# Queries of mixer B's second pair projected beside the last block's norm, high parts first in the feed-forward parts, and queries of mixer B split on POOL

## The chip, the core and the metric

The kernel runs on one core of a Trainium2 chip. The core has a matrix engine (TensorE, PE in the profile), three engines for elementwise work (VectorE or DVE, ScalarE or ACT, GpSimd or POOL), a queue engine that starts transfers (SyncE or SP), and 16 DMA engines. PE has a matmul row (PE) and a weight-load row (PEld). Each engine works through its own list of instructions in a fixed order; semaphores tie the lists together. The metric is device microseconds (us) of one execution, and lower is better. Medians of several runs are compared.

## What is computed

One layer of a streaming encoder for 1024 prompt frames and 32 sample frames, width 1024, in float32:

```python
h = adaln_in(x, gains[0], sh1, sc1)
x = x + FFN_RES * g1[:, None] * rmsnorm(swiglu(h, w1_gate, w1_up, w1_down), gains[1])
h = adaln_in(x, gains[2], sh2, sc2)
qa, ka, va, qb, kb, vb = jnp.split(h @ w_in, SPLITS, axis=-1)
oa, ob, rows = mixers(qa, ka, va, qb, kb, vb)
o = jnp.concatenate([rmsnorm(oa, ...), rmsnorm(ob, ...)], axis=-1) @ w_out
x = x + g2[:, None] * rmsnorm(o, gains[3])
h = adaln_in(x, gains[4], sh3, sc3)
x = x + FFN_RES * g3[:, None] * rmsnorm(swiglu(h, w2_gate, w2_up, w2_down), gains[5])
```

`swiglu(h) = (silu(h @ w_gate) * (h @ w_up)) @ w_down` with 2816 inner columns. Mixer A has 8 heads of 64 over 576 keys, mixer B has 8 query heads on 2 key heads with a window of 128 and a learned sink per head.

## The kernel before

The 1056 frames are held transposed (features on partitions, frames along the columns) in three **blocks** `tb` of 384, 384 and 288 columns. A float32 product is made of three faster matmuls: each operand is a high part plus a low part, and `mm3` (L324) issues, for one slice `k` of 128 features, weight-high times frame-high (L325), weight-high times frame-low (L326) and weight-low times frame-high (L327). `split_w` (L299) loads 128 weight columns, ACT copies out the high part (L303), DVE subtracts for the low part (L304). `norm_h` (L409) makes the two frame parts: DVE multiplies by the row factors into `n` (L420), ACT adds the shift and rounds to `h_hi` (L444), and the low part `h_lo` is made on DVE (L446) or, for every fourth slice, on POOL (L449). Ahead of it `mean_rstd` (L396) sums squares: ACT squares, POOL and DVE fold (`sq`, L368, L370), PE adds over partitions (`pss`, L357), DVE takes the inverse root (`rv`, `ry`, L334 to L391) and PE spreads it (`pr`, L405).

The stages are: first feed-forward part (`ffn`, key "h1"; in it `up(ff, tb)` makes the `gate` and `up` products of 128 inner columns, 24 matmuls each, and `down` the `dn` products); the norm `h2` and mixer B's keys, values and first queries, block by block (loop at L1077); attention; the output projection `wo`; second feed-forward part (key "h3").

In the attention stage 36 pieces for mixer B (32 `TileB`, 4 `TileS`) and 36 for mixer A run one after another. A `TileB` is two heads by 128 frames: `pre` (L796) clears part of a buffer `qs` on POOL (L799) and calls `split_q` (L716), which writes two copies of the query's high part (L721 or L723) and its low part (L724) for each of the two heads; `qk` makes the scores `Sb` (L813, L814), `tr` the transposes `ppb`, `av` the product with the values `po`. `SPLIT = "vav"` names the engines of the three writes: DVE, ACT, DVE. `TileS` are the sample frames' pieces (scores `Ss`). The four query projections of mixer B are `qk_proj` pieces (`pq`), 24 matmuls for each block: pair 0 is made in the loop at L1077, pairs 1 to 3 are the first units of `flows[0]`, whose work is spread as filler between the attention pieces 0 to 34, at a rate that is the units' summed cost over the pieces.

The order on each engine is fixed before the run by a scheduler: it gives earlier program steps priority and puts a later step ahead where it expects the earlier one to wait. Buffers come from pools by tag: `u` (6 buffers of block size, `u_tile`), `w` (8, weights), `r` (3, raw loads), `h` (5, among them `n`, `qs` and the transposed probabilities). PSUM has three banks for `p1` (gate, up, pv, pq, wo), two pairs for `p2` (dn, S, Sb, Ss) and one bank for `pc` (pss, pr, pk, po).

```python
                    for k in range(KT):
                        mm3(ps[s][:, :w], wgu[ff][s], k, hi[:, k, :], lo[:, k, :], k == 0, k == KT - 1)
```

Of the kernel before, what the change touches and what calls it, by code (L numbers as in the profile page):

```python
# [8 lines left out]
F32R = mybir.dt.float32r  # L9
# [8 lines left out]
KT = D // 128  # L18
# [40 lines left out]
PFILL = 5  # L59
KEARLY = 1  # L60
KB = 0
SPLIT = "vav"
LEAD_B = 2
MANUAL = False
WAIT = 3
# [1 line left out]
STAGES = ((0, 34), (37, 54))  # L67
# [7 lines left out]
def encoder_step(ctx: ExitStack, tc, x_prompt, x_sample, cache_a_k, cache_a_v, cache_b_k, cache_b_v,  # L75
# [4 lines left out]
    te, ve, ae, ge, dma = nc.tensor, nc.vector, nc.scalar, nc.gpsimd, nc.sync  # L80
# [215 lines left out]
        return bs  # L296


    def split_w(src):  # L299
        r = rpool.tile([128, 8, 128], F32, name="raw", tag="r")  # L300
        dma.dma_start(r, src)
        w = wpool.tile([128, 2, 8, 128], F32R, name="w", tag="w")
        ae.activation(w[:, 0], r, AF.Copy)  # L303
        ve.tensor_sub(w[:, 1], r, w[:, 0])  # L304
        return w

    def split_cols(wm, c):
        return split_w(wm[0, :, 128 * c:128 * c + 128].rearrange("(k p) n -> p k n", p=128))

    def split_rows(wm, r):  # L310
        return split_w(wm[0, 128 * r:128 * r + 128, :].rearrange("p (k n) -> p k n", n=128))
# [12 lines left out]
    def mm3(ps, w, k, hi, lo, start, stop):  # L324
        te.matmul(ps, w[:, 0, k], hi, start=start, stop=False)  # L325
        te.matmul(ps, w[:, 0, k], lo, start=False, stop=False)  # L326
        te.matmul(ps, w[:, 1, k], hi, start=False, stop=stop)  # L327


    def rsqrt(v, n, m):  # L330
# [170 lines left out]
    def need(key):  # L501
        while key not in done:
            step(1)
# [21 lines left out]
    def ffn(key, H, F, wg, wu, wd, per_group, key_out, after, beside=lambda ff, tb: None):  # L525
        late, pre = [], {}
        plan = rounds(*ROUNDS[key])
        begun = set()
        final = {tb: max(i for i, (g, t) in enumerate(plan) if tb in t) for tb in range(3)}

        def load(r, ff):
            pre[r, ff] = (split_cols(wg, ff), split_cols(wu, ff))

        load(0, 0)
        yield
        for r, (gi, blocks) in enumerate(plan):
            grp = GROUPS[gi]
            wgu, wds, gs = {}, {}, {}

            def up(ff, tb):  # L540
                need((key, tb))
                w = TB[tb][1]
                hi, lo = H[tb]
                ps = [p1("gate"), p1("up")]
                for s in range(2):
                    for k in range(KT):
                        mm3(ps[s][:, :w], wgu[ff][s], k, hi[:, k, :], lo[:, k, :], k == 0, k == KT - 1)
                    step(FAST if gi == 0 else PACE)
                sl = s_tile([128, 384], "sl")
                ae.activation(sl[:, :w], ps[0][:, :w], AF.Silu)  # L550
                ve.tensor_tensor(sl[:, :w], sl[:, :w], ps[1][:, :w], op=OP.mult)  # L551
                g = g_tile([128, 2, 384], "gg", F32R)
                ae.activation(g[:, 0, :w], sl[:, :w], AF.Copy)
                ve.tensor_sub(g[:, 1, :w], sl[:, :w], g[:, 0, :w])  # L554
                gs[ff, tb] = g
                beside(ff, tb)
                if late:
                    late.pop()()

            def down(tb, r=r, grp=grp, wds=wds, gs=gs):  # L560
                w = TB[tb][1]
                new = tb not in begun
                begun.add(tb)
                if new:
                    F[tb] = u_tile(tb, "facc", F32)
                if r == final[tb]:
                    if key_out != "y" or tb == 0:
                        finish()
                    own = marked((key_out, tb), after(tb))
                for mp in range(KT // 2):  # L570
                    ps = p2("dn")
                    for s in range(2):
                        for i, ff in enumerate(grp):
                            g = gs[ff, tb]
                            mm3(ps[:, s, :w], wds[ff], 2 * mp + s, g[:, 0, :w], g[:, 1, :w],
                                i == 0, i == len(grp) - 1)
                    o = F[tb][:, 2 * mp:2 * mp + 2, :]
                    if new:
                        ve.tensor_copy(o, ps[:, :, :w])
                    else:  # L580
                        ve.tensor_tensor(o, ps[:, :, :w], o, op=OP.add)  # L581
                    if r == final[tb]:
                        next(own)
                    step(1)
                if r == final[tb]:
                    side.append(own)

            x, y = grp
            if r:
                load(r, x)  # L590
            load(r, y)
            if r == XAT and key == "h1":
                XIN[1] = load_x(1)
            wgu.update({x: pre[r, x], y: pre[r, y]})
            for ff in grp:
                wds[ff] = split_rows(wd, ff)
            for tb in blocks:
                up(x, tb)
                up(y, tb)
                if len(begun) < 2:  # L600
                    down(tb)
                else:
                    late.append(lambda down=down, tb=tb: down(tb))
            if (gi, 2) == (gi, blocks[-1]):
                per_group(gi)
        late.pop()()
# [87 lines left out]
    def run(gen):  # L694
        for _ in gen:
            pass
# [378 lines left out]
        dma.dma_start(nbv_s[0, 0].rearrange("t h d -> t (h d)"), kvbs[:, 128:256])  # L1075

    for tb in range(3):  # L1077
        need(("h2", tb))
        if tb == 0:
            keys_cached()  # L1080
        for x in token_tiles(tb):
            run(kv_piece(*x))
        if tb == 2:
            KSB = wpool.tile([128, 2, 1024], F32R, name="KSB", tag="w")
            if PRIME:
                primed.append(load_qb(1))
            keys = [lambda: keys_new(0, 4), lambda: keys_new(4, 4), keys_sample]
        if tb == 2 and KEARLY == 1:
            keys.pop(0)()
        run(q0_piece(tb))  # L1090
        for i, x in enumerate(token_tiles(tb)):
            run(v0_piece(*x))
            if tb == 2 and KEARLY:
                keys and keys.pop(0)()
# [27 lines left out]
    def unit_qb(p):  # L1122
        return [(("B", p), lambda: load_qb(p), lambda w: flow_qb(p, w))]

    def unit_va(g):
        return [(("V", g), lambda: load_va(g), lambda w: flow_va(g, w))]

    def unit_qka(p):
        return [(("K", p), lambda: load_ka(p), lambda w: flow_ka(p, w)),
                (("A", p), lambda: load_qa(p), lambda w: flow_qa(p, w))]  # L1130

    flows = [(*STAGES[0], unit_qb(1) + unit_qb(2) + unit_qb(3) + unit_va(1) + unit_qka(0)),
             (*STAGES[1], unit_qka(1) + unit_qka(2) + unit_qka(3))]
    COST = {"B": 10.6, "V": 23.4, "K": 10.6, "A": 10.6}

# [78 lines left out]

        return LEAD_B if t < 36 else 1

    ready.add(("B", 0))
    todo = []
    for t in range(N):
        at = max(-1, t - lead(t))  # L1220
# [12 lines left out]
    with tc.manual_schedule(engines={mybir.EngineType.PE}) if MANUAL else ExitStack():  # L1233
        waits[0] = WAIT
        preps += [prepare(*key) for key in opens[0]]
        scores(-1, 1)
        if PRIME == 2:
            now = flow(flows[0][2])
            fill(PFILL)
# [116 lines left out]
```

## Time and profile before

| | before |
|---|---|
| median of 3 runs | 2216.33 us (2215.64 to 2218.37) |
| the profiled execution | 2217.6 us, its span 2215.8 us |
| granted TensorE clock, mean | 0.984 of full speed |
| PE busy | 2161.6 us (98%) |
| DVE, ACT, POOL busy | 1239.1 us (56%), 697.8 us (31%), 179.2 us (8%) |

The span is what lies between the first and the last instruction; 1.8 us of the profiled execution lie around it. PE is busy nearly throughout, so a microsecond counts where PE waits, where it runs at the lower of its two clock levels, or where work on it is removed. A wait stands in square brackets in the timeline, with what ended it. "PEclk" is the granted clock of a stretch, 1.00 being full speed (2.4 GHz) and 0.50 the lower level (1.2 GHz); a value between them is a stretch that had both.

### The profile page before, as it was taken

The numbers are of one execution on the slowest core, as the hardware profiler recorded it, in microseconds if no ns is written. First come the engines' busy times: TensorE is split into PE (matmuls) and PEld (weight loads), VectorE is DVE, ScalarE is ACT, GpSimd is POOL, SyncE is SP. The second block draws the span as 40 slices with busy tenths as digits, with TensorE's granted clock in tenths as the row PEclk, the third lists the DMA queues.
The fourth block names the chain that finished last, engine by engine and source line by source line (L and its number), as shares of the span: only waits on it lengthen the run. The fifth ranks groups of instructions, "written<-read, shape, count | busy, mean of one in ns | idle before, by whom it ended". The sixth has DMA issues, their size and how long they took to land.

```text
span 2215.8 us, 33976 instructions
## 1 busy us (share of the span) xinstructions
PE 2161.6 (98%) x14012; PEld 2068.6 (93%) x14012; DVE 1239.1 (56%) x2425; ACT 697.8 (31%) x1450; POOL 179.2 (8%) x281
## 2 busy tenths in 40 slices
PE   6999999999999999899999899999999999999998
PEld 4999999999999999799787589999999999999998
DVE  5788667874333497677444865785333333333336
ACT  4411111111121253576444663542111111111133
POOL 1100000000000023001110313220000000000000
PEclk8999999999999999899999899999999999999999
DMA  9253334434122352111112121424211111111122
GB/s 323 93 153 118 111 96 124 143 101 129 39 66 69 101 184 93 38 39 30 50 30 62 46 77 67 134 86 120 66 58 39 57 39 39 58 38 58 39 69 79
DMA packets 200623, 186.03 MB, mean 84 GB/s; under 512 B 7597, under 2 KB 169813, under 8 KB 199317
## 3 DMA queue, kind: packets, MB, share of 16 engines
q1 hardware_dynamic: 200468, 183.87, 27.1%
q8 instruction: 110, 1.80, 0.3%
q14 instruction: 45, 0.36, 0.1%
HBM read 164.12 MB, written 22.86 MB: 84 GB/s over the span
## 4 chain that ended last, share of the span: by engine, by line
PE 90%; DVE 4%; DMA 3%; ACT 1%; issue 1%; POOL 0%; SPq 0%; ACTq 0%; DVEq 0%; POOLq 0%
PE dn L325 7%; PE dn L326 7%; PE dn L327 7%; PE gate L327 7%; PE gate L326 7%; PE up L327 7%; PE up L326 7%; PE gate L325 7%; PE up L325 7%; PE po L713 3%; PE S L752 2%; PE pq L325 2%; PE pq L327 2%; PE pq L326 2%; DMA raw<-in_w_gate_dram 1%; PE pp L776 1%
## 5 line engine op out<-in xcount | busy, mean ns | idle before, releaser
L326 PE MATMUL gate<-h_lo,w 128*128 128x384 f32 (+1 forms) x1056 | 340.2, 322 | 4.0 <-DVE h_lo L446 4.0
L325 PE MATMUL dn<-gg,w 128*128 128x384 f32 (+1 forms) x1056 | 341.4, 325 | 1.1 <-DVE facc L581 1.0
L581 DVE TENSOR_TENSOR facc<-dn,facc 128x768 f32<-128x768 f32 (+1 forms) x240 | 212.9, 889 | 230.2 <-PE dn L327 229.9
L326 PE MATMUL dn<-gg,w 128*128 128x384 f32 (+1 forms) x1056 | 340.6, 323 | 0.6 <-DVE gg L554 0.6
L325 PE MATMUL gate<-h_hi,w 128*128 128x384 f32 (+1 forms) x1056 | 341.0, 323 | 0.0
L327 PE MATMUL gate<-h_hi,w 128*128 128x384 f32 (+1 forms) x1056 | 340.4, 322 | 0.0
L325 PE MATMUL up<-h_hi,w 128*128 128x384 f32 (+1 forms) x1056 | 340.2, 322 | 0.0
L326 PE MATMUL up<-h_lo,w 128*128 128x384 f32 (+1 forms) x1056 | 340.0, 322 | 0.0
L327 PE MATMUL dn<-gg,w 128*128 128x384 f32 (+1 forms) x1056 | 340.0, 322 | 0.0
L327 PE MATMUL up<-h_hi,w 128*128 128x384 f32 (+1 forms) x1056 | 339.9, 322 | 0.0
L304 DVE TENSOR_TENSOR w<-raw,w 128x1024 fp32r<-128x1024 f32 x187 | 231.5, 1246 | 150.5 <-ACT w L303 150.3
L303 ACT ACTIVATE w<-raw 128x1024 fp32r<-128x1024 f32 x187 | 195.7, 1056 | 266.1 <-PE dn L327 103.5
L550 ACT ACTIVATE sl<-gate 128x384 f32<-128x384 f32 (+1 forms) x132 | 60.9, 462 | 563.9 <-PE gate L327 560.9
L551 DVE TENSOR_TENSOR sl<-sl,up 128x384 f32<-128x384 f32 (+1 forms) x132 | 68.5, 519 | 292.1 <-PE up L327 286.1
L326 PEld LDWEIGHTS gate<-h_lo,w 128*128 128x128 f32 x1056 | 198.6, 188 | 4.6 <-DVE h_lo L446 4.6
L325 PEld LDWEIGHTS dn<-gg,w 128*128 128x128 f32 x1056 | 199.2, 189 | 1.6 <-DVE facc L581 1.2
L326 PEld LDWEIGHTS dn<-gg,w 128*128 128x128 f32 x1056 | 199.2, 189 | 1.0 <-DVE gg L554 0.9
L327 PEld LDWEIGHTS dn<-gg,w 128*128 128x128 f32 x1056 | 199.1, 189 | 0.0
L325 PEld LDWEIGHTS gate<-h_hi,w 128*128 128x128 f32 x1056 | 198.7, 188 | 0.1
L327 PEld LDWEIGHTS gate<-h_hi,w 128*128 128x128 f32 x1056 | 198.7, 188 | 0.0
L327 PEld LDWEIGHTS up<-h_hi,w 128*128 128x128 f32 x1056 | 198.7, 188 | 0.0
L325 PEld LDWEIGHTS up<-h_hi,w 128*128 128x128 f32 x1056 | 198.5, 188 | 0.0
(224 smaller groups left out, 3367.4 us busy)
## 6 DMA issues: line engine op xcount, KB each, us to landing
raw<-in_w_mod_dram SPq DMA_DIRECT2D x56, 512.0 KB, 4.0
raw<-in_w_gate_dram SPq DMA_DIRECT2D x54, 512.0 KB, 4.0
raw<-in_w_up_dram SPq DMA_DIRECT2D x54, 512.0 KB, 4.7
raw<-in_w_down_dram SPq DMA_DIRECT2D x54, 512.0 KB, 4.5
raw<-in_w_in_dram SPq DMA_DIRECT2D x18, 512.0 KB, 4.3
wm<-in_w_mod_dram SPq DMA_DIRECT2D x8, 1024.0 KB, 7.4
raw<-in_w_out_dram SPq DMA_DIRECT2D x13, 512.0 KB, 4.5
xr<-xs SPq DMA_DIRECT2D x16, 384.0 KB, 3.5
```

The lines of the kernel that those rows point to most:

```text
L303: ae.activation(w[:, 0], r, AF.Copy)
L304: ve.tensor_sub(w[:, 1], r, w[:, 0])
L325: te.matmul(ps, w[:, 0, k], hi, start=start, stop=False)
L326: te.matmul(ps, w[:, 0, k], lo, start=False, stop=False)
L327: te.matmul(ps, w[:, 1, k], hi, start=False, stop=stop)
L550: ae.activation(sl[:, :w], ps[0][:, :w], AF.Silu)
L551: ve.tensor_tensor(sl[:, :w], sl[:, :w], ps[1][:, :w], op=OP.mult)
L581: ve.tensor_tensor(o, ps[:, :, :w], o, op=OP.add)
L713: te.matmul(po[64 * h:64 * h + 64, :n], vsl(j, h, kn), PT(h, j, kn), start=j == 0, stop=j == nt - 1)
L752: te.matmul(S[:, c:ce], self.T[:, h, :], KQ[:, 0, 128 * k0 + c:128 * k0 + ce], start=True, stop=True)
L776: te.transpose(pp[:, j - j0, :], P[:, 128 * j:128 * j + 128], ident)
```

## The change

Three edits. `up` no longer calls `mm3` per slice but `mm_all`: for all eight slices weight-high and weight-low times frame-high, and after them weight-high times frame-low; the 24 matmuls are the same. Pair 1 of mixer B's queries is taken out of `flows[0]`: its weights are loaded in the loop at L1077 ahead of the wait for the third block's norm, into a buffer of the pool `u` (named `wu`), blocks 0 and 1 are projected there, and block 2 after the first scores of the attention stage. `SPLIT = "ggg"` puts all three writes of `split_q` on POOL.

```diff
-SPLIT = "vav"
+SPLIT = "ggg"
...
-    def split_w(src):
+    def split_w(src, pool=None):
         r = rpool.tile([128, 8, 128], F32, name="raw", tag="r")
         dma.dma_start(r, src)
-        w = wpool.tile([128, 2, 8, 128], F32R, name="w", tag="w")
+        if pool is None:
+            w = wpool.tile([128, 2, 8, 128], F32R, name="w", tag="w")
+        else:
+            w = pool.tile([128, 2, 8, 128], F32R, name="wu", tag="u", bufs=6)
         ae.activation(w[:, 0], r, AF.Copy)
         ve.tensor_sub(w[:, 1], r, w[:, 0])
         return w
...
+    def mm_all(ps, w, hi, lo):
+
+        for k in range(KT):
+            te.matmul(ps, w[:, 0, k], hi[:, k, :], start=k == 0, stop=False)
+            te.matmul(ps, w[:, 1, k], hi[:, k, :], start=False, stop=False)
+        for k in range(KT):
+            te.matmul(ps, w[:, 0, k], lo[:, k, :], start=False, stop=k == KT - 1)
...
                 for s in range(2):
-                    for k in range(KT):
-                        mm3(ps[s][:, :w], wgu[ff][s], k, hi[:, k, :], lo[:, k, :], k == 0, k == KT - 1)
+                    mm_all(ps[s][:, :w], wgu[ff][s], hi, lo)
                     step(FAST if gi == 0 else PACE)
...
     for tb in range(3):
+        if tb == 2:
+            q1_piece = start_qb(1, split_cols(w_in, 13, upool))
+            for b in range(2):
+                for _ in q1_piece(b):
+                    step(2)
         need(("h2", tb))
...
-    flows = [(*STAGES[0], unit_qb(1) + unit_qb(2) + unit_qb(3) + unit_va(1) + unit_qka(0)),
+    flows = [(*STAGES[0], unit_qb(2) + unit_qb(3) + unit_va(1) + unit_qka(0)),
...
-    ready.add(("B", 0))
+    ready |= {("B", 0), ("B", 1)}
...
         scores(-1, 1)
+        run(q1_piece(2))
```

How the order moves, at three places. **First**, PE at the start of block 1 in the first feed-forward part, right behind the `dn` products of block 0 (`gate_771`, `up_772` and `gate_827` are three PSUM banks, `h_hi_456` and `h_lo_457` block 1's parts). Before:

```order
L325 MATMUL gate_771<-h_hi_456,w_258 128x384
L325 MATMUL up_772<-h_hi_456,w_263 128x384
L325 MATMUL gate_827<-h_hi_456,w_315 128x384
L326 MATMUL gate_771<-h_lo_457,w_258 128x384
L327 MATMUL gate_771<-h_hi_456,w_258 128x384
```

Now:

```order
L335 MATMUL gate_771<-h_hi_456,w_258 128x384
L336 MATMUL gate_771<-h_hi_456,w_258 128x384
L335 MATMUL up_772<-h_hi_456,w_263 128x384
L336 MATMUL up_772<-h_hi_456,w_263 128x384
L335 MATMUL gate_827<-h_hi_456,w_315 128x384
L336 MATMUL gate_827<-h_hi_456,w_315 128x384
```

Three matmuls stood ahead of the first low part; now 36 on high parts and 20 `dn` matmuls do. The second feed-forward part has the same two orders at its block 1, with other buffer numbers.

**Second**, PE at the end of the loop at L1077 (`pv_7977` is the last value product of block 1, `pss_7670`, `pr_7759` the sums and factors of block 2's norm, `h_hi_7789` its output). Before:

```order
L671 MATMUL pv_7977<-w_7467,h_lo_7136 128x256
L357 MATMUL pss_7670<-ones_98,sq_7700 128x1 x2
L357 MATMUL pss_7670<-ones_98,sq_7700 32x1
L357 MATMUL pss_7670<-ones_98,sq_7736 128x1 x2
L357 MATMUL pss_7670<-ones_98,sq_7736 32x1
L405 MATMUL pr_7759<-ident_96,ry_7747 128x128 x2
L405 MATMUL pr_7759<-ident_96,ry_7747 128x32
L669 MATMUL pv_8003<-w_7447,h_hi_7789 128x256
```

Now, around the sums:

```order
L330 MATMUL pq_8009<-h_hi_6700,wu_8005 128x384
L328 MATMUL pq_8035<-h_hi_7135,wu_8005 128x384
L368 MATMUL pss_7670<-ones_98,sq_7700 128x1 x2
L368 MATMUL pss_7670<-ones_98,sq_7700 32x1
L368 MATMUL pss_7670<-ones_98,sq_7736 128x1 x2
L368 MATMUL pss_7670<-ones_98,sq_7736 32x1
L329 MATMUL pq_8035<-h_lo_7136,wu_8005 128x384
L330 MATMUL pq_8035<-h_hi_7135,wu_8005 128x384
```

and around the factors:

```order
L329 MATMUL pq_8035<-h_lo_7136,wu_8005 128x384
L330 MATMUL pq_8035<-h_hi_7135,wu_8005 128x384
L416 MATMUL pr_7759<-ident_96,ry_7747 128x128 x2
L416 MATMUL pr_7759<-ident_96,ry_7747 128x32
L679 MATMUL pv_8061<-w_7447,h_hi_7789 128x256
```

25 of the 48 moved matmuls stand ahead of the sums, 23 between the sums and the factors. Behind the factors PE's order is as before: six `pv` on the first high parts, then `pk`.

**Third**, POOL around the same norm (`qs` are the split queries of the first attention pieces). Before:

```order
L799 MEMSET qs_8245 64x256
L449 TENSOR_TENSOR h_lo_7790<-n_7830,h_hi_7789 128x256
L449 TENSOR_TENSOR h_lo_7790<-n_7830,h_hi_7789 128x32
L799 MEMSET qs_8273 64x256
L799 MEMSET qs_8301 64x256
L449 TENSOR_TENSOR h_lo_7790<-n_7910,h_hi_7789 128x256
```

Now:

```order
L809 MEMSET qs_8303 64x256
L733 CAST qs_8303<-qbt_7472 64x128 x4
L734 TENSOR_TENSOR qs_8303<-qbt_7472,qs_8303 64x128 x2
L460 TENSOR_TENSOR h_lo_7790<-n_7830,h_hi_7789 128x256
L460 TENSOR_TENSOR h_lo_7790<-n_7830,h_hi_7789 128x32
L809 MEMSET qs_8331 64x256
L733 CAST qs_8331<-qbt_7472 64x128 x4
L809 MEMSET qs_8386 64x256
L733 CAST qs_8386<-qbt_7472 64x128 x4
L460 TENSOR_TENSOR h_lo_7790<-n_7910,h_hi_7789 128x256
```

Each piece now has seven POOL instructions where it had one, and two pieces' copies stand ahead of block 2's last low part.

## Rows read from the trace of the kernel before

**Rows 1.** Page, part 1: the matmul row and the weight loads, busy us and counts.

```profile
PE 2161.6 (98%) x14012; PEld 2068.6 (93%) x14012; DVE 1239.1 (56%) x2425; ACT 697.8 (31%) x1450; POOL 179.2 (8%) x281
```

**Rows 2.** Windows: stretch, length, busy PE, PEld, DVE, ACT, POOL, then PEclk, DMA, GB/s.

```profile
75.00:80.00 5.00, 5.00 (x22) 5.00 (x21) 5.00 (x7) 1.88 (x3) 2.58 (x3) 0.67 0.01 3
885.00:900.00 15.00, 9.53 (x55) 8.47 (x55) 11.75 (x45) 8.43 (x27) 3.33 (x7) 0.66 0.00 0
920.00:925.00 5.00, 4.47 (x18) 3.90 (x19) 4.34 (x15) 3.28 (x14) 0.31 (x1) 0.66 0.17 55
1440.00:1450.00 10.00, 7.87 (x37) 7.55 (x36) 10.00 (x14) 5.57 (x10) 3.80 (x4) 0.83 0.11 29
920.00:1063.00 143.00, 141.53 (x1109) 128.26 (x1109) 107.47 (x382) 99.03 (x348) 11.45 (x40) 0.99 0.10 29
```

**Rows 3.** PE timeline (start, us, instruction, wait) where block 1 starts, both feed-forward parts.

```profile
71.73 0.34 PE L325 MATMUL up<-h_hi,w 128*128 128x384 f32 x1
71.90 0.34 PE L325 MATMUL gate<-h_hi,w 128*128 128x384 f32 x1
74.07 0.45 PE L326 MATMUL gate<-h_lo,w 128*128 128x384 f32 x1 [1.83 <-DVE h_lo L446]
...
1440.46 0.34 PE L325 MATMUL gate<-h_hi,w 128*128 128x384 f32 x1
1442.92 0.45 PE L326 MATMUL gate<-h_lo,w 128*128 128x384 f32 x1 [2.13 <-DVE h_lo L446]
```

**Rows 4.** DVE timeline ahead of the first of these two waits.

```profile
68.66 4.29 DVE L420 SCALAR_TENSOR_TENSOR n<-xt,acoef,pr 128x384 f32<-128x384 f32 x8
72.86 1.16 DVE L446 SCALAR_TENSOR_TENSOR h_lo<-n,modT,h_hi 128x384 fp32r<-128x384 f32 x1
```

**Rows 5.** PE timeline at block 2's norm, then at the first attention scores.

```profile
884.45 1.34 PE L357 MATMUL pss<-ones,sq 128*128 128x1 f32 x12
888.24 1.75 PE L405 MATMUL pr<-ident,ry 128*128 128x128 f32 x6 [2.44 <-DVE ry L338]
891.11 0.58 PE L669 MATMUL pv<-w,h_hi 128*128 128x256 f32 x1 [1.11 <-ACT h_hi L444]
...
894.66 1.08 PE L1057 MATMUL pk<-ident,vt 128*128 128x128 f32 x4 [1.91 <-DVE n L420]
...
917.93 0.22 PE L877 MATMUL Ss<-KB2s,qbs 64*32 64x32 f32 x2
920.53 0.39 PE L813 MATMUL Sb<-KSB,qs 128*128 128x256 f32 x1 [2.38 <-ACT Ps L888]
```

**Rows 6.** DVE timeline at block 2's norm.

```profile
884.19 0.46 DVE L370 TENSOR_TENSOR sq<-sq 128x288 f32<-128x288 f32 x1
885.83 0.16 DVE L388 TENSOR_SCALAR rv<-pss 128x2 f32<-128x2 f32 x1 [1.19 <-PE pss L357]
...
890.03 4.49 DVE L420 SCALAR_TENSOR_TENSOR n<-facc,acoef,pr 128x256 f32<-128x256 f32 x16 [1.94 <-PE pr L405]
```

**Rows 7.** Page, part 5: the split of weights on DVE, busy us and mean ns.

```profile
L304 DVE TENSOR_TENSOR w<-raw,w 128x1024 fp32r<-128x1024 f32 x187 | 231.5, 1246 | 150.5 <-ACT w L303 150.3
```

**Rows 8.** Who writes `qs`: ns min/median/max, first and last start, forms.

```profile
L721 ACT ACTIVATE qs<-qbt x64: 307/309/312, 891.3 to 1053.6; 64x128 fp32r<-64x128 f32 x64
L723 DVE CAST qs<-qbt x64: 198/223/652, 895.0 to 1052.3; 64x128 fp32r<-64x128 f32 x64
L724 DVE TENSOR_TENSOR qs<-qbt,qs x64: 260/285/720, 898.2 to 1053.0; 64x128 fp32r<-64x128 f32 x64
```

**Rows 9.** POOL by line and shape: busy us, mean ns, idle before.

```profile
L742 POOL COPY qz<-KQ 64x128 f32<-64x128 f32 x64 | 22.9, 358 | 2.8
L799 POOL MEMSET qs<- 64x256 f32 x32 | 10.2, 318 | 141.9 <-PE po L713 68.8 <-PE Sb L814 44.6 <-ACT vt L673 4.2
L449 POOL TENSOR_TENSOR h_lo<-n,h_hi 128x256 fp32r<-128x256 f32 x6 | 5.4, 903 | 51.5 <-ACT n L448 51.5
L449 POOL TENSOR_TENSOR h_lo<-n,h_hi 128x32 fp32r<-128x32 f32 x6 | 2.3, 377 | 0.0
```

More of the change, by code (lines that the diff above doesn't have):

```diff
@@ L305, in split_w, with split_cols @@
         return w
-    def split_cols(wm, c):
-        return split_w(wm[0, :, 128 * c:128 * c + 128].rearrange("(k p) n -> p k n", p=128))
+    def split_cols(wm, c, pool=None):
+        return split_w(wm[0, :, 128 * c:128 * c + 128].rearrange("(k p) n -> p k n", p=128), pool)
     def split_rows(wm, r):
```

## The prediction

> **What bounds the kernel now.** I read the page's busy times first. PE is busy 2161.6 of 2215.8 us [rows 1], so a change pays only where PE waits, where it runs at the lower clock, or where work beside a wait is moved. Next, the windows show the stretches with a clock below 1.00 [rows 2], and in them the PE timeline shows which wait stands there. Three kinds of place bear on the change. Block 1 of both feed-forward parts waits 1.83 and 2.13 us for a low part [rows 3]. Block 2's norm before attention has waits of 2.44, 1.11 and 1.91 us in fifteen microseconds, and the start of attention one of 2.38 us [rows 5]. The rest of mixer B's stage has next to none: 141.53 of 143 us busy at 0.99 of full clock, with DVE at 107.47, ACT at 99.03 and POOL at 11.45 us [rows 2]. A lower clock costs twice: over 5 us busy at 0.67, 5.00 × 0.33 = 1.65 us of full-speed work is lost beside the wait itself.
>
> **High parts first.** At block 1 PE issues three matmuls on the high part and then needs the low part's first slice, which DVE makes only when its eight products `n` are through (4.29 us), 1.16 us a slice [rows 4]; so PE waits 1.83 us. Afterwards 36 matmuls on high parts and 20 `dn` stand ahead of it. Two matmuls of 384 columns start 71.90 − 71.73 = 0.17 us apart [rows 3], so the 36 alone last 36 × 0.172 = 6.2 us, three times the wait. DVE, which makes six of the eight low parts (POOL the two others) at 1.16 us each or less, began them at 72.86, so they are through by about 80; PE's 36 and the 20 `dn`, 9.6 us in all from 71.7 on, reach past that. What is late next: the last high parts, made by ACT slice after slice; the 20 `dn` lie among them. Gain: the wait and the lost clock, 1.83 + 1.65 = 3.5 us, and in the second part 2.13 + 7.87 × 0.17 = 1.3, 3.4 us. **Together −7.** The number of matmuls is the same. At the very first block, which has no `dn` work, 24 high matmuls stand ahead of the lows in place of few; a wait there could shrink or grow by about the size of those above; I take nothing and keep ±2 for the range.
>
> **The second pair's queries: out of the filler.** 48 matmuls of 384 columns and 24 of 288 leave the stage of mixer B: 48 × 0.172 = 8.3, 24 × 0.172 × 0.75 = 3.1 us, in sum **−11.4** if PE limits that stage, as 141.53 of 143 us says [rows 2]. The filler is thinner for it: the rate is the units' cost over the pieces. The stage would be some 131.5 us, in which DVE would be busy for 107 and ACT for 99 even if the split stayed on them. PE stays the bound. I put 1 us against it for waits that thinner filler lets through (between 0 and 6): **−10.4**.
>
> **Into the norm hole.** 25 of the 48 stand ahead of the sums `pss`, which start at 884.45, right behind DVE's last fold (884.19 + 0.46 = 884.65) [rows 5, 6]. They begin 25 × 0.172 = 4.3 us later. Then 23 × 0.172 = 4.0 us stand between `pss` and the factors `pr`, where PE waited 2.44: the chain from `pss` through `rv` and `ry` is covered. `pr` so starts at 884.45 + 4.3 + 1.3 + 4.0 ≈ 894, in place of 888.24. Behind `pr` nothing changed: DVE's `n` (4.49 us [rows 6]) follow `pr`, and PE waits 1.11 and 1.91 us as before. `pr` took 1.75 us for six, at the lower clock; having run without a stop ahead, it may now take half, −0.9. So `pk` starts at 894 + (894.66 − 888.24) − 0.9 ≈ 899.4 instead of 894.66: **+4.7** for 8.3 us of moved work. Bounds: if all 48 only fill waits, +8.3 − 2.44 − 1.11 − 1.91 = +2.8; if nothing is filled, +8.3.
>
> Other instructions of the move: one raw load (SP), one ACT copy and one DVE subtraction of 1.25 us [rows 7] for `wu`; these leave the filler and come near block 1's projections instead, where the order puts them between block 1's low parts. PE has `pv` and `pk` work there, no wait of its timeline in that stretch; and `pss` has its 4.3 us of slack. SP's queue is moved past nothing that PE waits for. Cost nothing; up to 1.3 us if DVE's piece shifts block 2's folds. `wu` holds one of six `u` buffers until block 2's piece is done.
>
> **At the start of attention** block 2's piece, 24 × 0.129 = 3.1 us, stands behind the first scores. There PE waits 2.38 us for ACT's `Ps`, then runs at 0.66 for 4.47 us of work, a loss of 1.5 [rows 2, 5]. The piece covers the wait, +3.1 − 2.4 = +0.7, and if the clock holds, −1.5. The first `Sb` needs `qs`, now from POOL; I add 0.6 for that being late: **−0.2** (without that −0.8; with neither wait nor clock covered +3.1).
>
> **Queries split on POOL.** Per `TileB` two ACT copies of 309 ns, two DVE casts of 223 and two DVE subtractions of 285 ns go [rows 8]: 32 × 0.62 = 19.8 us off ACT, 32 × 1.02 = 32.5 us off DVE, both beside PE. I count no gain for it. POOL gets, for each piece, the memset (318 ns), four copies and two subtractions. No row has these; a POOL copy of the same shape takes 358 ns, and the subtractions lie between its 377 (32 columns) and 903 ns (256 columns) [rows 9]. At 128 columns I take 0.57, by proportion between these: 0.32 + 4 × 0.36 + 2 × 0.57 = 2.9 us a piece. Low bound: copies at 0.22 as on DVE, subtractions at 0.38, 2.0 us; high: copies at 0.65 and subtractions at 0.90, 4.7 us. A piece of mixer B has (143 − 11.4) / 32 = 4.1 us of PE's time, so POOL at 2.9 follows, one piece ahead, and its lag hides: **0**. What hides it is the buffering of the next piece's `qs`; the copies of two pieces also stand ahead of block 2's last low part in POOL's order, 2.9 us each, but these last lows are used at the end of the `pv` products, behind 1.91 us waiting and `pk`; up to 2 us if they are late.
>
> **A rule against this edit.** DVE's casts into `qs` take 223 ns at the median and 652 at most, its subtractions 285 and 720 [rows 8]: something holds single instructions 0.43 us. The Trainium skill's page "SBUF — State Buffer", section "Who interferes with whom", says that DVE and GpSimd share one port pair as an exclusive lock, held for the whole instruction, and that a DVE copy in a two-port mode or a DVE instruction with two inputs in SBUF blocks against a GpSimd instruction. By it the maxima are collisions, agreeing in kind with the rows, and a POOL busy 70% of mixer B's stage would meet many more; DVE's and POOL's instructions would stretch both. Its result is the third case below.
>
> **Sum.** −7 − 10.4 + 4.7 − 0.2 = −13 against the profiled 2217.6 us, which is 1.3 us above the median of 2216.3: **2203** as a median.
>
> **The rivals.**
> Slower: *POOL becomes the bound of mixer B's stage.* If each of the six copies and subtractions is stretched by the 0.43 us that the maxima show (652 − 223 ns [rows 8]), a piece takes 2.9 + 6 × 0.43 = 5.5 us and 32 of them 176 us, 45 above 131.5; it decides from 4.1 us on. With two thirds of the instructions hit, 4.8 us: 32 × (4.8 − 4.1) = 22 us, 2203 + 22 = **2225**. For it: the maxima, and that each `Sb` needs its `qs`. Against: the median is not stretched, POOL's own copies of 64×128 have a mean of 358 ns beside a busy DVE [rows 9], and DVE loses 32.5 us of work there. Chance 0.10.
> Same: *mixer B's stage isn't bound by PE.* The filler fills it to 141.53 us, because the scheduler spread it so; the chain scores, exponentials, transposes, products may last as long without it. Then the removal gives nothing: −7 + 4.7 − 0.2 = −2.5, **2214**. For it: DVE is busy for 75% and ACT for 69% of the stage [rows 2], and each piece's chain passes both. Against: both lose work, and pieces overlap. Chance 0.13.
> Faster by less: *the wait goes on with the low part.* If high parts first only move the wait to ACT's last high part, the edit gives 0 and the rest −6: **2210**. For it: ACT rounds slices one after another behind the same `n`. Against: 36 high matmuls and 20 `dn` pass three banks in which those parts come one by one. Chance 0.09.
>
> **How the numbers follow.** The forecast, 2203, has 0.68. Its own range comes from the bounds. Downwards: −2 at the first block, −1.9 in the hole, −0.6 at attention's start, −1 for filler that lets no wait through, −1.5 if the freed DVE and ACT end the waits left in mixer B's stage (143 − 141.5), and −0.7 for the median's own spread, in sum −7.7. Upwards: +2, +3.6, +3.3 and +5, in sum +14, of which I take a little over half, since they don't hang together: 2195 to 2211. The range of 8 in 10 adds the third rival and the second, which end at 2210 and 2214, and leaves out 2225: **2195 to 2214**. A measurement here can tell about 0.2%, 4.4 us, from no change, so faster is under 2211.9 and slower over 2220.8: faster 0.68 + 0.09 = 0.77, same 0.13, slower 0.10.
>
> **What the profile after would show.** No wait for `h_lo` at 74 and 1443 us, and a clock of 1.00 there. 48 `pq` ahead of `pr`, which starts near 894 less the 3.5 us gained before, with the waits for `h_hi` and `n` behind it unchanged. Mixer B's stage near 131 us, PE still over 95% busy; POOL about 93 us busy there, no PE wait on `qs`, no stretch of its copies above 0.4 us. DVE about 32 us less, ACT 20 less. What makes me wrong: a PE wait on `qs` in every piece (POOL), waits on `Sb` or `ppb` that take the filler's place (same), or a wait for `h_hi` where `h_lo` stood.

## The result and the profile after

The changed kernel takes 2221.26 us in the median of 13 runs (2217.92 to 2225.33), the kernel before, run beside it, 2214.48 (2209.75 to 2218.47): ratio 1.0031, 95% interval 1.0021 to 1.0042. It is slower by about 7 us; 2203, 13 us faster, was forecast. The profiled execution took 2220.24 us, its span 2218.3 us, mean granted clock 0.988. Since that span is only 2.5 us above the one of before, some 4 us of the difference between the medians stand in no comparison of these two traces; ratios below come from the medians, places from the traces.

The page after, part 1, answers to [rows 1]:

```profile
PE 2159.1 (97%) x14012; PEld 2065.9 (93%) x14012; DVE 1211.0 (55%) x2297; ACT 678.0 (31%) x1386; POOL 250.2 (11%) x473
```

DVE lost 28 us, ACT 20, POOL gained 71: the split moved, and PE has as many matmuls as before. The windows of the changed kernel, the same five stretches and columns as in [rows 2]:

```profile
75.00:80.00 5.00, 5.00 (x31) 5.00 (x30) 5.00 (x8) 4.04 (x8) 1.87 (x2) 1.00 0.02 7
885.00:900.00 15.00, 13.43 (x89) 12.84 (x87) 7.05 (x24) 5.16 (x14) 4.94 (x10) 1.00 0.19 79
920.00:925.00 5.00, 5.00 (x43) 4.42 (x42) 1.34 (x3) 0.98 (x2) 0.00 (x0) 1.00 0.62 204
920.00:1063.00 143.00, 133.40 (x1027) 118.27 (x1026) 81.16 (x259) 77.30 (x272) 69.60 (x201) 0.98 0.11 33
1440.00:1450.00 10.00, 9.77 (x60) 9.45 (x60) 8.17 (x25) 5.84 (x11) 1.81 (x2) 1.00 0.00 0
```

These four short windows all show full clock now, 0.67, 0.66, 0.66 and 0.83 before. But the work in the second and third has moved by 7.5 and 8 us, so their places have to be looked at again:

```profile
900.00:910.00 10.00, 7.84 (x52) 7.41 (x53) 5.79 (x20) 4.23 (x14) 6.95 (x17) 0.83 0.01 2
```

Right behind the norm hole the clock still falls, for a loss of 10 × 0.17 = 1.7 us where 15 × 0.34 = 5.1 were lost before. The start of attention, now from 925 to 935 us, is at 1.00. Against that, mixer B's stage has 9.6 us without PE (window 920:1063; 1.5 before), although DVE, ACT and POOL are each busy for less than 60% of it. The clearest way to see where time went is to compare the start of the same matmul in both traces. "Behind" is the changed kernel's start less that of before:

| point in PE's list | before, us | behind, us |
|---|---|---|
| first `dn` (end of the first block's start) | 66.66 | +4.5 |
| 135th `dn` (block 1 well begun) | 138.73 | +0.5 |
| a `pv` near block 1's end | 878.57 | +2.4 |
| second `pk` (norm hole over) | 894.66 | +7.5 |
| first `Ss` | 916.64 | +8.3 |
| ninth `Sb` | 921.22 | +10.1 |
| first `pkc` (end of mixer B's stage) | 1065.62 | +10.7 |
| last `wo` | 1414.04 | +8.4 |
| near the end of the `dn` | 2197.29 | +2.6 |

The forecast wanted the stage from the ninth `Sb` to the first `pkc`, called **the B stretch** below, to become shorter by some 10 us; it became 0.6 us longer. In this stretch the waits of PE in the changed kernel are (engine, line, what it waited for: us in all, times, longest; `Pb` are the exponentials of a piece's scores, `o` its products as ACT copies them out):

```profile
PE Sb L823 <- ACT Pb L834: 2.9, 3, 1.7
PE po L723 <- ACT o L715: 1.8, 2, 1.3
PE ppb L852 <- ACT Pb L840: 1.7, 5, 0.6
PE Sb L823 <- POOL qs L733: 1.2, 2, 0.9
PE Sb L823 <- POOL qs L734: 1.1, 2, 0.8
...
```

Before, there were 1.8 us for `o` and a DMA's 1.1. Waits are spread over the whole chain of a piece, and only 2.3 us of them name POOL's `qs`.

### The profile page after: what moved, and what is told of

It is laid out like the page before. It is cut to its first block, busy times and chain, and to the rows that moved or that the text cites. A ratio compares the mean times of both kernels' runs of the same rounds, so it can differ in the third digit from the quotient of the medians.

```text
span 2218.3 us, 33928 instructions
## 1 busy us (share of the span) xinstructions
PE 2159.1 (97%) x14012; PEld 2065.9 (93%) x14012; DVE 1211.0 (55%) x2297; ACT 678.0 (31%) x1386; POOL 250.2 (11%) x473
## 4 chain that ended last, share of the span: by engine, by line
PE 88%; DVE 5%; DMA 3%; ACT 2%; issue 1%; POOL 1%; SPq 0%; DVEq 0%; ACTq 0%; POOLq 0%
PE up L338 7%; PE up L335 7%; PE dn L328 7%; PE gate L338 7%; PE dn L330 7%; PE dn L329 7%; PE up L336 7%; PE gate L335 7%; PE gate L336 7%; PE S L762 2%; PE po L723 2%; PE pq L328 2%; PE pq L330 2%; PE pq L329 2%; PE pv L681 1%; PE pv L679 1%
## 5 line engine op out<-in xcount | busy, mean ns | idle before, releaser
L335 PE MATMUL up<-h_hi,w 128*128 128x384 f32 (+1 forms) x1056 | 331.6, 323 | 0.0
L335 PE MATMUL gate<-h_hi,w 128*128 128x384 f32 (+1 forms) x1056 | 331.5, 323 | 0.0
L336 PE MATMUL up<-h_hi,w 128*128 128x384 f32 (+1 forms) x1056 | 330.9, 321 | 0.0
L336 PE MATMUL gate<-h_hi,w 128*128 128x384 f32 (+1 forms) x1056 | 330.5, 321 | 0.0
L379 POOL TENSOR_TENSOR sq<-sq 128x384 f32<-128x384 f32 (+1 forms) x48 | 51.4, 1080 | 1486.7 <-ACT sq L375 1461.4
L338 PE MATMUL gate<-h_lo,w 128*128 128x384 f32 (+1 forms) x1056 | 195.7, 321 | 0.0
L338 PE MATMUL up<-h_lo,w 128*128 128x384 f32 (+1 forms) x1056 | 191.8, 321 | 0.0
```

Source lines behind the costliest of these rows:

```text
L335: te.matmul(ps, w[:, 0, k], hi[:, k, :], start=k == 0, stop=False)
L336: te.matmul(ps, w[:, 1, k], hi[:, k, :], start=False, stop=False)
L338: te.matmul(ps, w[:, 0, k], lo[:, k, :], start=False, stop=k == KT - 1)
L379: e.tensor_tensor(sq[:, 0, :w], sq[:, 0, :w], sq[:, 1, :w], op=OP.add)
```

## The experiments

**Parts alone.** First each of the three edits by itself, and the change without its third.

*e1_hi*, the first edit alone (with `mm_all` as in the change):

```diff
-                    for k in range(KT):
-                        mm3(ps[s][:, :w], wgu[ff][s], k, hi[:, k, :], lo[:, k, :], k == 0, k == KT - 1)
+                    mm_all(ps[s][:, :w], wgu[ff][s], hi, lo)
```

> The kernel before with high parts first in `up` alone. In the trace of the changed kernel the first block lost 5 us (from 0.4 us ahead of the kernel before at 44 us to 4.5 behind at 67), block 1 of each feed-forward part won about 3.5. If these belong to this edit, PE shows a new wait of about 3 us for the first block's h_hi near 50 us, no wait for h_lo at 74 and 1443 us, and the time is 2 to 3 us under before (ratio 0.9987, 0.998 to 1.000). Rival: the first block's loss comes from elsewhere (DMA); then no new wait there and 7 us under before (0.997).

Measured: 2212.01 us beside 2216.43, ratio 0.9978 (0.9968 to 0.9988), a little faster than expected. The new wait is there, where 0.26 us stood before. PE timeline of this kernel:

```profile
52.33 1.94 PE L625 MATMUL pt<-ident,X 128*128 128x128 f32 x16 [2.40 <-ACT h_hi L449]
```

and of the changed kernel, where the matmuls behind it took 3.41 us in place of 1.94, at a lower clock (0.83 from 50 to 60 us):

```profile
52.72 3.41 PE L627 MATMUL pt<-ident,X 128*128 128x128 f32 x16 [3.17 <-ACT h_hi L451]
```

*e5_hi_later*: `mm_all` only where `tb` is not 0, `mm3` in block 0.

> The kernel before with high parts first in `up` from block 1 on; block 0 keeps the old order. High parts first in every block measured 0.9978, and its trace was behind the kernel before by 2.4 us at the first dn product (67 us). If that loss is block 0's (24 matmuls on four slices are done before the other four slices come, 36 were ready in the old order), it goes away, the gains at 74 and 1443 us stay, and the time is 2 to 3 us lower still: ratio 0.9967 (0.9955 to 0.9975). Rival: block 0's order costs nothing over the whole run; then 0.9978 again.

Measured: 2207.38 us beside 2216.73, 0.9962 (0.9949 to 0.9974). That is the value expected if the loss is block 0's. The intervals of e1 and e5 overlap, so the 3.5 us between their ratios (0.0016 × 2216) stand on the traces too: at the first `dn` this kernel is level with before, e1 2.4 us behind, and PE waits at that place for 0.44 us, for a DMA. In block 0 only four slices of the frame parts are there at first. The old order finds 36 matmuls on them in three banks, the new one 24, since the other 12 are on low parts, which now stand behind the high parts of slices not yet made.

*e2_q1*, the moved queries alone (`SPLIT` as before, `mm3` in `up`):

> The kernel before with the move of pair 1's queries alone; the split stays on DVE, ACT, DVE and `up` as it was. Theory S (the split on POOL took the gain back): the norm hole costs 5 us and the start of attention 2 as in the changed kernel, but mixer B's stage is about 9 us shorter, so 2 us under before (ratio 0.999, 0.997 to 1.000), with PE waits of under 3 us in that stage. Theory F (thinner filler lets as many waits through as it removes work): mixer B's stage as long as before, 5 to 7 us over before (ratio 1.003), with 6 us more of PE waits in that stage and none of them on qs.

Measured: 2217.93 us beside 2216.43, 1.0005 (0.9996 to 1.0014). In its trace the norm hole cost 5.1 us (1.1 ahead of before at block 1's `pv`, 4.0 behind at the second `pk`), the start of attention 1.8, and the B stretch became 8.8 us shorter. That is theory S's length for the stretch, not its total: the three come to −2 us, and the median says +1.1 (−0.9 to +3.1).

*e3_split*, the third edit alone:

```diff
-SPLIT = "vav"
+SPLIT = "ggg"
```

> The kernel before with the three writes of the split on POOL alone; the filler is as thick as before. Theory S: POOL takes 2.5 to 2.8 us in a row for each piece's queries, and PE waits for qs or for what follows it even behind thick filler: 3 to 8 us over before (ratio 1.001 to 1.004). Theory F: thick filler covers it, no change within 2 us (0.999 to 1.001).

Measured: 2226.62 us beside 2216.43, 1.0043 (1.0031 to 1.0056), +9.5 us, just above the range of theory S. The split is the loss, with the thick filler too (pair 1's queries still in it). Yet of the 4.6 us without PE in e3's B stretch no wait names `qs`: 2.6 are for a DMA, 1.7 for ACT's `Pb`, 0.2 for ACT's `o`. *e8_program_order_split* is, whatever its label says, this same kernel once more, in a single run:

> The split on POOL alone, one more look at the trace of the kernel that measured 1.0043: the stretch from the ninth Sb to the first pkc again about 6 us longer than in the kernel before with about as much waiting on PE, or, if the first look was a chance, no longer than before.

Measured: 2225.39 us, and the B stretch 150.01 us in place of 150.17, so the first trace was no accident.

*e4_hi_q1*, the change with `SPLIT = "vav"`:

> The changed kernel with the split back on DVE, ACT, DVE. Theory S: mixer B's stage is 8 us or so shorter than in the changed kernel, total 4 to 6 us under before (ratio 0.9975). Theory F: no shorter than in the changed kernel, 3 to 6 us over before (ratio 1.002).

Measured: 2213.66 us beside 2216.43, 0.9986 (0.9976 to 0.9995): 3 us under before, where theory S expected 4 to 6, with a B stretch 9.5 us shorter than the changed kernel's. From here to the change, 1.0031, is one string, and 10 us. The parts multiply to 0.9978 × 1.0005 × 1.0043 = 1.0026; the whole measured 1.0031.

**What in the split costs?** The B stretch of four kernels, as windows with the columns of [rows 2]. Before:

```profile
921.22:1065.62 144.40, 141.50 (x1115) 128.17 (x1114) 107.52 (x382) 99.38 (x348) 11.45 (x40) 0.99 0.11 32
```

the split alone (e3):

```profile
923.69:1073.86 150.17, 145.62 (x1115) 130.25 (x1114) 85.08 (x265) 83.06 (x290) 71.93 (x208) 0.97 0.10 30
```

high parts and queries without the split (e4):

```profile
929.14:1064.68 135.54, 131.15 (x1043) 117.00 (x1042) 105.80 (x384) 97.36 (x345) 11.37 (x40) 0.99 0.11 31
```

and the whole change:

```profile
931.28:1076.27 144.99, 133.48 (x1042) 118.40 (x1042) 84.08 (x268) 81.55 (x288) 71.43 (x208) 0.98 0.10 29
```

In each pair PE has the same matmuls, and POOL, at 72 us of 145 to 150, is far from a bound. The split costs 5.8 us in the first pair (1.6 more without PE; 2.3 more lost to the lower clock, added over thirty parts of the stretch; 1.8 more of full-speed time on PE), 9.5 in the second (7.1, 1.6, 0.8). In the second pair that is as much as the spans differ (9.1 us); e3 also loses 2.1 us ahead of this stretch, from block 1's last `pv` on, and 2.5 behind it, up to the first `wo`, which nothing below follows.

The waits do not say that POOL is late: with the split on DVE and ACT, e4's waits name `qs` for 2.6 us in three places, with the split on POOL the changed kernel's for 2.3. What differs within each pair is the order of PE's list. The four `Sb` matmuls of a piece stand together in the kernel before: in none of 32 pieces do eight or more other matmuls stand between the first and the last. In e4 that is so in 1 piece, in e3 in 6, in the change in 13. (Counted in the planned list, where a matmul like `po` is one instruction; the trace shows it as two.) PE timeline of the changed kernel, rows of `Sb`:

```profile
971.01 0.28 PE L823 MATMUL Sb<-KSB,qs 128*128 128x256 f32 x1
...
973.04 0.28 PE L824 MATMUL Sb<-KSB,qs 128*128 128x256 f32 x1
973.16 0.28 PE L823 MATMUL Sb<-KSB,qs 128*128 128x256 f32 x1
...
974.96 0.28 PE L824 MATMUL Sb<-KSB,qs 128*128 128x256 f32 x1
...
975.32 0.28 PE L823 MATMUL Sb<-KSB,qs 128*128 128x256 f32 x1
...
978.70 0.36 PE L823 MATMUL Sb<-KSB,qs 128*128 128x256 f32 x1 [0.78 <-POOL qs L734]
```

and POOL's timeline beside it:

```profile
975.31 0.31 POOL L809 MEMSET qs<- 64x256 f32 x1 [2.53 <-PE Sb L824]
975.66 1.34 POOL L733 CAST qs<-qbt 64x128 fp32r<-64x128 f32 x4
977.07 0.98 POOL L734 TENSOR_TENSOR qs<-qbt,qs 64x128 fp32r<-64x128 f32 x2
978.11 0.31 POOL L809 MEMSET qs<- 64x256 f32 x1
```

One piece's four matmuls are 4 us apart, with projections between them. POOL's next piece stands 2.53 us idle until the last of them has freed a buffer, and the filler that could have covered what comes next is already used. Then the list asks for further pieces' scores one behind the other, faster than POOL's 2.8 us a piece (975.31 to 978.11), and PE waits (0.78 us here and 0.29 at the next piece). This is one place, and the other waits were not followed. Two theories fit it: **L**, POOL hands the queries over late, whatever the order; **O**, it is the list, cut up for the sake of queries that the scheduler expects late, that costs. They differ where PE's list is held still.

*e7_program_order*, the kernel before with PE's attention stages as the program is written:

```diff
-MANUAL = False
+MANUAL = True
```

> The base for the next kernel: the kernel before with PE's order in the attention stages as the program is written, not rearranged. Slower than before, by anything from 1 to 5 per cent; nothing hangs on how much.

Measured: 2237.66 us beside 2216.73, 1.0095 (1.0082 to 1.0109), just under what was expected. *e9_program_order_ggg*, the same with `SPLIT = "ggg"`; PE's list in the B stretch is the same matmul for matmul, while the lists of the other engines are planned as ever:

> The split on POOL in the kernel whose attention stages keep the program's order on PE, so that PE's list of mixer B's stage is the same with either split (the base measured 1.0095). Theory L (POOL hands the queries over late, whatever the order): PE waits for qs, and the stage from the ninth Sb to the first pkc is 5 us or more longer than the base's; ratio 1.012 to 1.015. Theory O (POOL keeps up; what costs is that PE's order comes out cut into smaller pieces): that stretch within 2 us of the base's, no waits on qs to speak of, ratio 1.009 to 1.011.

Measured: 2234.02 us beside 2215.86, 1.0078 (1.0064 to 1.0092). The B stretch of e7 and its waits (beside a DMA's 3.1 us),

```profile
928.49:1072.44 143.95, 136.16 (x1081) 121.94 (x1080) 105.00 (x367) 97.42 (x337) 11.22 (x39) 1.00 0.11 31
```

```profile
PE ppb L842 <- ACT Pb L830: 4.4, 5, 1.5
```

and of e9, where the DMA's 3.3 us are all the waiting:

```profile
929.95:1067.71 137.76, 134.49 (x1080) 121.84 (x1080) 82.44 (x255) 81.22 (x281) 70.82 (x201) 1.00 0.11 33
```

With its list held still, the split on POOL made the stretch 6.2 us shorter: PE no longer waits for ACT's `Pb`, and never for `qs`. Theory L is out for thick filler. Theory O's numbers missed too, on the other side: it expected the stretch within 2 us of e7's and a ratio of 1.009 or more, and had no gain in it. With the change's thin filler, where PE had waited for `qs`, the same pair:

*e12_order_change_vav* is e4 with `MANUAL = True`:

> High parts first and the moved queries, split on DVE, ACT, DVE, with PE's attention stages in the program's order: the base for the next. Between 1.005 and 1.012 of the kernel before, by the 1.0095 of the same order without the two edits. Theory O (the split's cost is the order that comes out for it): mixer B's stage, ninth Sb to first pkc, 133 to 138 us here. Theory L doesn't speak of this base.

*e13_order_change_ggg* is the whole change with `MANUAL = True`:

> The whole change with PE's attention stages in the program's order, so that PE's list in mixer B's stage is that of the base sent with it, and the filler is thin as in the change. Theory O: with thin filler too the split on POOL costs nothing: the stretch from the ninth Sb to the first pkc is 0 to 6 us shorter than the base's, the ratio to the kernel before at or under the base's. Theory L (late queries show once the filler is thin): that stretch 4 us or more longer than the base's, with waits of PE on qs.

Measured: 2226.12 us, 1.0049 (1.0034 to 1.0064), and 2221.77 us, 1.0031 (1.0018 to 1.0043), both beside 2215.71. The B stretch of e12 and what PE waited for most in it,

```profile
931.16:1066.96 135.80, 126.08 (x1008) 111.81 (x1008) 103.66 (x370) 96.66 (x334) 11.33 (x39) 0.99 0.11 31
```

```profile
PE ppb L852 <- ACT Pb L840: 6.1, 7, 1.7
```

and the B stretch of e13:

```profile
933.76:1061.79 128.03, 123.27 (x1009) 110.21 (x1008) 81.88 (x257) 80.06 (x277) 69.38 (x201) 1.00 0.12 33
```

7.8 us shorter with the split, a little more than the 6 us expected; PE's waits for `Pb` on ACT fell from 6.1 us to 0.3, and in e13 none is for `qs`. So POOL can carry the split beside either filler. As ratios the two pairs overlap at their intervals' ends: that the split gains on a fixed list is shown in the stretch, not in the whole time. The change in plain program order is as fast as in the order planned for it (1.0031 both), although its B stretch is 17.0 us shorter: the program's order loses that again behind this stretch.

**Two more ways at the split.** *e10_split_early*, each piece's `pre` two pieces ahead:

> The split on POOL with each piece's clearing, copies and subtractions put two pieces ahead in the program instead of one, from the same five buffers; nothing else (the split alone measured 1.0043). Theory L: the queries come earlier, most of the loss goes, ratio 1.000 to 1.002. Theory O: another order again, but lateness was not the cost: 1.003 to 1.006.

Measured: 2218.65 us beside 2215.86, 1.0010 (1.0001 to 1.0019). That is in theory L's range, not O's: as I had put O, lateness didn't matter at all. With e9 and e13 beside it another reading is open, argued and not shown: moving the queries ahead in the program moves them ahead for the scheduler as well, so that the list comes out better. The B stretch came out at 146.76 us with 2.5 us of waiting. It still has 9 pieces cut up, while e3, with 6, measured 1.0043: the number of cut pieces alone doesn't measure what a list costs.

*e11_sub_on_pool*, `SPLIT = "vag"`:

> The kernel before with only the two low parts of the split on POOL; the copies stay on DVE and ACT. POOL's share of a piece falls from 2.5 to 1.3 us. Theory L: the loss falls with the length of POOL's part, to a half or less: ratio 1.000 to 1.002. Theory O: the order comes out different again and the loss doesn't follow POOL's time: anything from 0.999 to 1.005, with the loss in the trace standing in more changes between kinds of matmul and in the clock, not in waits on qs.

Measured: 2218.37 us beside 2215.86, 1.0013 (1.0004 to 1.0022). It lies in both ranges. In its trace the B stretch is 144.64 us, with no piece cut up, as before; the 2.5 us of the medians stand nowhere in the trace that I can name.

**The moved queries.** *e6_q1_behind*: the same move, written behind block 2's norm.

```diff
         need(("h2", tb))
+        if tb == 2:
+            for b in range(2):
+                run(q1_piece(b))
```

> The move of pair 1's queries alone, but blocks 0 and 1 stand behind block 2's norm in the program, so that the order puts them where PE waits for the norm and not ahead of its sums. With the move as in the change pk was 5.1 us later than before and the ratio was 1.0005. If the 25 matmuls ahead of pss are what costs there, pk comes only 2.5 to 3.5 us later than before and the ratio falls to 0.9995 or less (0.998 to 1.000). Rival: a later pss isn't the cost, the moved matmuls are; then pk is 5 us later again and the ratio 1.0005.

Measured: 2216.33 us beside 2216.73, 0.9998 (0.9989 to 1.0008), but it tells nothing of its question: the order came out as in e2, 25 matmuls ahead of `pss` and 23 behind, and `pk` 5.1 us later. Whether a later `pss` is what costs there stays open.

*e14_hi_later_q1*, e5 and the moved queries:

> High parts first from block 1 on and the moved queries, split on DVE, ACT, DVE. If the parts add (0.9962 and 1.0005), 0.9967 (0.9955 to 0.998): no better than high parts first from block 1 on alone. Rival: the moved queries pay once the first block's loss is away, under 0.995.

Measured: 2205.57 us beside 2215.71, 0.9959 (0.9946 to 0.9971). That fits parts that add, and the rival's gain did not come; it beats both kernels, and so does e5, 0.9962, with less of a change.

## Why the prediction was wrong

**High parts first: right in its mechanism, 2 us off in sum.** Both waits for `h_lo` are gone and the clock stays up, and where the second feed-forward part starts, e1 goes from 3.7 to 8.1 us ahead of before, 4.4 against 3.4 forecast (block 1 of the first part: 4.0 in the changed kernel, against 3.5). The step that failed is "a wait there could shrink or grow; I take nothing": block 0 lost 2.4 us (e1) to 5 us (the changed kernel) at the first `dn`. I had counted 24 high matmuls there, and not set beside them the 36 that the old order had ready.

**The norm hole: right.** +4.7 forecast, +5.1 in both traces (2.4 to 7.5, −1.1 to +4.0). In the changed kernel, as said, `pss` moved behind 25 `pq`, the wait for `ry` went, and the two behind `pr` stayed (1.11 and 1.91 in [rows 5]):

```profile
890.97 0.33 PE L328 MATMUL pq<-h_hi,wu 128*128 128x384 f32 x1
891.15 1.34 PE L368 MATMUL pss<-ones,sq 128*128 128x1 f32 x12
...
896.52 0.94 PE L416 MATMUL pr<-ident,ry 128*128 128x128 f32 x6
898.57 0.39 PE L679 MATMUL pv<-w,h_hi 128*128 128x256 f32 x1 [1.11 <-ACT h_hi L455]
...
902.13 0.63 PE L1067 MATMUL pk<-ident,vt 128*128 128x128 f32 x4 [2.59 <-DVE n L431]
```

`pr` at 0.94 us for 1.75 is the clock that the sum took back as 0.9; 0.7 us went again into a longer wait for `n` (2.59 for 1.91), since DVE's chain is as long as before.

**The start of attention: +1.8 for −0.2.** The wait for `Ps` fell only from 2.38 to 0.53 us under 3.1 us of projection. In the changed kernel:

```profile
930.59 0.39 PE L823 MATMUL Sb<-KSB,qs 128*128 128x256 f32 x1 [0.53 <-ACT Ps L898]
```

The clock did stay up there. But the 1.5 us counted for it lie mostly behind the ninth `Sb` (920 to 925 us before), so they belong to the B stretch as measured here, and e4 ran at the lower clock in its B stretch as well, at another place:

```profile
1020.00:1025.00 5.00, 4.83 (x20) 4.86 (x21) 4.43 (x19) 3.77 (x14) 0.31 (x1) 0.66 0.01 2
```

That is 0.66 again over five microseconds: the recovered 1.5 us were given back.

**The thinner filler: −8.9 for −10.4**, without the split (e4 against before). Full-speed work on PE fell by 10.4 us (not 11.4) and time without PE rose by 1.5. The second rival, a stage not bound by PE, falls with e4. Both together make the moved queries worth nothing: −5.9 forecast, +1.1 ± 2 measured. Of the 7 us, 0.4 lie in the hole, 2 at the start, 1.5 in the stretch; 3 stand only in the median. By e14 beside e5 (0.9959 for 0.9962) the move is worth −0.7 us, between the −2 of the trace and the +1.1 of the median; the intervals leave it open.

**The split: the step that failed.** "POOL at 2.9 follows, one piece ahead, and its lag hides: 0": this term, put at nothing, cost 10 us (e4 against the change). POOL's own time in it was right. The tile `qs` in the changed kernel, columns as in [rows 8]:

```profile
L733 POOL CAST qs<-qbt x128: 282/292/1274, 893.0 to 1060.6; 64x128 fp32r<-64x128 f32 x128
L734 POOL TENSOR_TENSOR qs<-qbt,qs x64: 446/454/1331, 894.5 to 1061.5; 64x128 fp32r<-64x128 f32 x64
```

With the memset's 0.31 a piece takes 0.31 + 4 × 0.30 + 2 × 0.48 = 2.5 us by the means of the stretch (2.8 from start to start, with the gaps), not 2.9, and POOL was busy for 70 us of the stage, not 93. The slower rival, POOL as the bound from 4.1 us on, did not happen. That its 2225 lies near the 2221 measured is luck: it named the side on which the time fell, not the mechanism, and by its own terms two thirds of six instructions come to 2.9 + 4 × 0.43 = 4.6 us, not 4.8. What the sum lacked is that PE's list is planned anew when the queries come from another engine. I had read the order of the norm and of the feed-forward parts, where the edits stand, and not of mixer B's stage, where a one-word edit moves no code. There 13 pieces had their scores pulled apart, which the order shows before any run. Shown, by e9 and e13, is that POOL's work by itself is not the cost: on a list that stays as it is, the split on POOL makes the stretch 6.2 and 7.8 us shorter, so the 10 us come only with the list planned for it. Not shown is the new list by itself: no run has the change's list with its queries made on DVE and ACT, so the loss may need both, the cut-up list and POOL's queries. Why the scheduler cuts the list up (what it takes POOL's instructions to last) is in no trace either.

## What to carry to other kernels

Where a scheduler plans the order, moving work to another engine is two changes, the work and the list; compare the lists of every stage that uses the result, and run the pair on a fixed list before blaming the engine. Work put into a hole ahead of the chain that makes the hole delayed that chain here by all of itself (25 matmuls, 4.3 us, ahead of `pss`), while the 23 behind the chain's start filled the wait for `ry`; whether all 48 behind it would have been cheaper, no run shows. High parts first pays where the low parts come late. Where the slices themselves arrive in two halves, as in block 0, it runs dry sooner, so count what each order has ready.

## What the runs showed of the hardware

**Some changes of kind on PE cost about a tenth of a microsecond.** `pv`, `pq` and `Sb` work on high and low parts, `ppb` and `po` on plain float32, and `po` also with another tile (`128*64` in its row). The kernel before, PE timeline, `pv` around a `ppb` and a `po`:

```profile
993.39 0.62 PE L842 MATMUL ppb<-ident,Pb 128*128 128x128 f32 x4
993.77 0.36 PE L669 MATMUL pv<-w,h_hi 128*128 128x256 f32 x1
993.98 0.28 PE L670 MATMUL pv<-w,h_hi 128*128 128x256 f32 x1
994.09 0.29 PE L671 MATMUL pv<-w,h_lo 128*128 128x256 f32 x1
994.31 0.66 PE L713 MATMUL po<-PTb,vt 128*64 128x128 f32 x8
994.90 0.39 PE L669 MATMUL pv<-w,h_hi 128*128 128x256 f32 x1
995.12 0.28 PE L670 MATMUL pv<-w,h_hi 128*128 128x256 f32 x1
995.24 0.28 PE L671 MATMUL pv<-w,h_lo 128*128 128x256 f32 x1
```

The next matmul starts 0.12 us after a `pv` of 256 columns (995.12 to 995.24), but 0.21 after one right behind a `ppb` and 0.22 after one right ahead of or behind a `po`. The same holds for `Sb`; between `pv`, `pq` and `Sb` there is none, and none right ahead of a `ppb` (an `Sb` at 955.93 us, `ppb` at 956.05). Which property of `ppb` and `po` costs the time, these rows don't separate. A list cut into smaller pieces pays a little for it: between the two groups e3 changes 117 times in the B stretch against 109 before, some part of its 1.8 us more of full-speed time. It is a small part of the loss, for e10 has 117 as well.

**POOL is held by DVE, but rarely.** POOL in the changed kernel, four copies that take 1.34 us elsewhere (975.66 above):

```profile
937.91 2.32 POOL L733 CAST qs<-qbt 64x128 fp32r<-64x128 f32 x4
```

and DVE at that moment:

```profile
938.15 1.22 DVE L323 TENSOR_TENSOR w<-raw,w 128x1024 fp32r<-128x1024 f32 x1 [0.62 <-ACT w L322]
```

One of the four copies took 1.27 us and ended just after the subtraction, which has two inputs. It is the blocking that the Trainium skill's page "SBUF — State Buffer", section "Who interferes with whom", states, and the trace agrees in kind, with a maximum of 1274 ns beside a median of 292. But such rows are few: 9 of the 192 copies and subtractions are longer than their median by more than 0.07 us, by 3 us in all. As a price for this kernel the rule came to next to nothing.
